# Moving a query block and the early input loads within the order of the projection stage of a hybrid attention / RWKV-7 / MoE block

## The chip, the cores and the metric

One core of a Trainium2 chip runs the whole program. The metric is the device time of one execution in microseconds; each version is given by the median of its runs, with the smallest and the largest beside it.

## What is computed

One layer of an encoder over 2048 tokens of width 1024, cut to what matters here:

```python
h = rmsnorm(x, g_mix) * (1 + sc1) + sh1          # adaLN: sh1, sc1 come from c @ w_ada
pq, pk, pv, pr = split(h @ w_in)                 # one combined input projection
q, k = rope(rmsnorm(pq)), rope(rmsnorm(pk))      # 8 query heads, 2 key heads, 64 wide
o_att = softmax(q @ k.T / 8) @ pv                # all 2048 keys, grouped queries
r, k, v, dw, da, dg = split(centred_shift(pr))   # p + mu * ((prev + next) / 2 - p)
kk = k * k_k / |k * k_k|                         # per head
for each direction:                              # forward and backward
    w  = exp(-0.606531 * sigmoid(w0 + tanh(dw) @ w_up))
    a  = sigmoid(a0 + da @ a_up)
    kd = k * (1 + (a - 1) * k_a)
    y += wkv7_scan(r, w, kd, v, kk, a)           # recurrence over the tokens
    bonus += sum(r * kd * r_k) * v
o_rwkv = (groupnorm(y) * ln_w + ln_b + bonus) * (sigmoid(dg) @ g_up)
x = x + gt1 * concat(o_att, o_rwkv) @ w_out
h2 = rmsnorm(x, g_ffn) * (1 + sc2) + sh2
x = x + gt2 * expert_choice_ffn(h2)              # 16 experts, each takes 256 tokens
```

## The kernel before

The program has stages: the projections (`phase1`), the mixers, in which attention blocks and the recurrence's chunks are interleaved, the output projection, the router and the experts. A mixer's first instructions need the projections' last rows, through DRAM buffers (`d_qk`, `d_x`, `d_v` and others).

**Projections.** `phase1` works on the tokens in two halves of 1024. Of a half, the normalised, modulated input lies on chip transposed, in four pieces of 256 tokens (`hh`, `hl`, a high and a low part, since each product is made of three fp32r products). `project` (L239 to L248) makes 128 output columns for one piece: 8 slices of the inner dimension times 3 products, 24 matmuls (L247) into one PSUM tile `proj_ps`; there are three such buffers. A projection of 128 columns is four of these, 96 matmuls, with weights loaded by `load_w` on SP's queue and split by ScalarE (L148) and GpSimd (L149, `w_lo`). `plain` copies the result out; `shifted` also makes the token shift: one ScalarE row (L263) and two VectorE rows (L265) per piece.

After the key projection and two shifted ones for the decay, rate and gate inputs (blocks 12 and 13), which `phase1` writes out at the start of each half, come the items of a list:

- `q0` to `q3`, **query blocks** (`qk`): four plain projections and `qk_post` (L309), which normalises per head and applies the rotary factors. Its large VectorE rows are L324, L328 and L329, two of each.
- `h0` to `h3`, **recurrence blocks** (`heads`): three shifted projections (`s_r`, `s_k`, `s_v`, 12 pieces) and `prep` (L356), for two quarters of 512 tokens. `prep` begins with head sums on TensorE (`pn`, L275), which become the factor `pb` (L306) of the first VectorE row that all else needs: L378, `kkn`. Then it makes the operands of the recurrence for both directions. Its end is L422 (`pinv`, the last reader of `s_r`), the matmuls `pbo` (L424) and `pg` (L428), and the VectorE rows L426 and L432.
- `x0` to `x2`, **early inputs** (`early`): the next half's `x` for one piece, four loads of 128x512, with their sums of squares on ScalarE (L162), the reciprocal root on VectorE (L165, L166, L55 to L63) and the scaling. `load_xp(half, 3)` follows within v0.
- `v0`, **values** (`values`): a plain projection; in the first half it also makes the second half's pieces (`load_piece`), piece by piece, with that half's key projection.

```python
X_TAGS = [x.split() for x in ("rrkk vvrk vrkv rrkk", "rkrk vrkv vrkv rrkk")]     # L30
xt = self.tpool.tile([P, 512], F32, tag="s_" + tags[2 * i + m], name="xt", bufs=4)   # L159
pair = lambda tag: [self.tpool.tile([P, 512], F32, tag=tag, name=tag, bufs=5 if tag == "p" else 4) for _ in range(2)]
for item in ORDER[half]:                                                         # L579
    dict(q=qk, h=heads, v=values, x=early)[item[0]](int(item[1]))
```

The loads of `x` use buffers of the recurrence blocks: x0 of the second half takes two of the four `s_r` and two of the four `s_k` buffers (tags "rkrk"). A block takes two of each of `s_r`, `s_k` and `s_v`, so two blocks' tiles exist at a time; buffers go round in the order in which the program asks for them.

The order of the list is that in which the instructions are written. A scheduler then places each engine's instructions, by priority and by when their inputs are expected, so that neighbouring items overlap on the engines. On the chip each engine runs its row of instructions in that fixed order, and so does SP's queue.

Of the kernel before, what the change touches and what calls it, by code (L numbers as in the profile page):

```python
# [24 lines left out]
CH = 64  # L25
DSC = 0.606531

ORDER = [x.split() for x in ("h0 q0 h1 q1 h2 h3 x0 q2 x1 q3 x2 v0", "h0 q0 h1 q1 h2 q2 h3 v0 q3")]

X_TAGS = [x.split() for x in ("rrkk vvrk vrkv rrkk", "rkrk vrkv vrkv rrkk")]  # L30

# [6 lines left out]
class Encoder:  # L38
# [397 lines left out]
    def phase1(self):  # L436
# [13 lines left out]
        with ExitStack() as c:  # L450
# [72 lines left out]
            for half in range(2):  # L523
# [54 lines left out]
                ahead, xts = [], []  # L578
                for item in ORDER[half]:  # L579
                    dict(q=qk, h=heads, v=values, x=early)[item[0]](int(item[1]))  # L580
# [1034 lines left out]
```

## Time and profile before

| | before |
|---|---|
| runs (us) | 3757.07, 3762.44, 3744.38 |
| median | 3757.07 |
| profiled execution, its own time | 3751.49 |
| span of its profile | 3749.8 |
| TensorE busy | 94% |
| VectorE busy | 67% |
| mean granted TensorE clock | 0.957 |

The profile is of one execution. Engines are PE (TensorE's matmuls), PEld (its weight loads), DVE (VectorE), ACT (ScalarE), POOL (GpSimd) and SP (the engine that issues most DMAs); busy times are in microseconds and `x` counts instructions. The span is also shown in 40 equal slices, of which each digit is the busy share in tenths; a slice is 93.7 us long, so the projection stage, some 760 us, is the first eight. PEclk is the TensorE clock that was granted, as a share of full speed. In the views of single instructions a row is: start, length, engine, line, operation, result <- operands, shape, and in square brackets how long the engine had been idle before it and what ended that. In the groups by line a row is: line, engine, operation, count | busy time, mean ns of one | idle time just before them, and what ended most of it.

### The profile page before, as it was taken

The numbers are of one execution on the slowest core, as the hardware profiler recorded it, in microseconds if no ns is written. First come the engines' busy times: TensorE is split into PE (matmuls) and PEld (weight loads), VectorE is DVE, ScalarE is ACT, GpSimd is POOL, SyncE is SP. The second block draws the span as 40 slices with busy tenths as digits, with TensorE's granted clock in tenths as the row PEclk, the third lists the DMA queues.
The fourth block names the chain that finished last, engine by engine and source line by source line (L and its number), as shares of the span: only waits on it lengthen the run. The fifth ranks groups of instructions, "written<-read, shape, count | busy, mean of one in ns | idle before, by whom it ended". The sixth has DMA issues, their size and how long they took to land. (4 is left out here: it accounts for less than half of the span.)

```text
span 3749.8 us, 61495 instructions
## 1 busy us (share of the span) xinstructions
PE 3509.9 (94%) x23436; PEld 2856.7 (76%) x23436; DVE 2516.7 (67%) x4289; ACT 1755.2 (47%) x3066; POOL 1512.5 (40%) x1484
## 2 busy tenths in 40 slices
PE   6998899799999999999999997993999999999998
PEld 5887788656666666676666664772999999999997
DVE  6688778876857778558867675447555656655653
ACT  4445444414555555545555564231444444444443
POOL 3445344526263353663364554332332332322321
PEclk8999899879999999999999998996999999999999
DMA  5335334443323433433333232443566766767664
GB/s 182 105 130 168 112 113 141 139 129 73 91 68 79 121 95 85 114 88 87 84 85 85 69 82 82 156 145 113 188 206 205 222 202 216 218 203 222 220 199 127
DMA packets 531228, 510.93 MB, mean 136 GB/s; under 512 B 213304, under 2 KB 449954, under 8 KB 525812
## 3 DMA queue, kind: packets, MB, share of 16 engines
q1 hardware_dynamic: 520612, 472.08, 41.1%
q0 software_dynamic: 10000, 34.91, 4.0%
q8 instruction: 185, 3.03, 0.3%
q14 instruction: 111, 0.91, 0.1%
q10 hardware_dynamic: 320, 0.00, 0.0%
HBM read 392.57 MB, written 109.07 MB: 134 GB/s over the span
## 5 line engine op out<-in xcount | busy, mean ns | idle before, releaser
L1452 DVE TENSOR_TENSOR w_lo<-w_raw,w_hi 128x2048 fp32r<-128x2048 f32 x189 | 432.3, 2293 | 385.8 <-ACT w_hi L1449 385.4
L1516 PE MATMUL gu<-hh,w_lo 128*128 128x256 f32 x2048 | 573.5, 280 | 0.0
L1516 PE MATMUL gu<-hl,w_hi 128*128 128x256 f32 x2048 | 572.7, 280 | 0.0
L1516 PE MATMUL gu<-hh,w_hi 128*128 128x256 f32 x2048 | 572.5, 280 | 0.0
L699 POOL TENSOR_TENSOR acc<-acc,pt 128x512 f32<-128x512 f32 x256 | 354.9, 1391 | 469.0 <-ACT pt L696 456.0
L1449 ACT CAST w_hi<-w_raw 128x2048 fp32r<-128x2048 f32 x192 | 366.9, 1912 | 319.9 <-PE down L1539 133.3
L696 ACT ACTIVATE pt<-st_ps 128x1024 f32<-128x1024 f32 x256 | 262.2, 1024 | 394.8 <-PE st_ps L695 221.2
L649 DVE TENSOR_REDUCE mx<-s_ps 128x1 f32<-128x512 f32 x512 | 342.6, 681 | 149.7 <-PE s_ps L648 148.2
L247 PE MATMUL proj_ps<-hh,w_hi 128*128 128x258 f32 (+1 forms) x1280 | 375.3, 294 | 32.8 <-DVE s_k L265 23.8
L1516 PEld LDWEIGHTS gu<-hh,w_lo 128*128 128x128 f32 x2048 | 388.0, 189 | 0.0
L1516 PEld LDWEIGHTS gu<-hh,w_hi 128*128 128x128 f32 x2048 | 385.6, 188 | 1.3
L1516 PEld LDWEIGHTS gu<-hl,w_hi 128*128 128x128 f32 x2048 | 385.5, 188 | 1.4
L247 PE MATMUL proj_ps<-hl,w_hi 128*128 128x258 f32 (+1 forms) x1280 | 373.0, 292 | 6.4 <-DVE hl L149 5.9
L247 PE MATMUL proj_ps<-hh,w_lo 128*128 128x258 f32 (+1 forms) x1280 | 371.5, 290 | 0.0
L149 POOL TENSOR_TENSOR dl<-hid,dh 128x256 fp32r<-128x256 f32 x128 | 135.1, 1056 | 448.1 <-ACT dh L148 447.8
L686 PE MATMUL o_ps<-pt,av 128*64 128x512 f32 x1024 | 278.5, 627 | 6.7 <-ACT pt L696 6.7
L247 PEld LDWEIGHTS proj_ps<-hh,w_hi 128*128 128x128 f32 x1280 | 250.8, 196 | 41.7 <-issue 23.0
L247 PEld LDWEIGHTS proj_ps<-hl,w_hi 128*128 128x128 f32 x1280 | 251.4, 196 | 10.6 <-DVE hl L149 6.6
L699 DVE TENSOR_TENSOR acc<-acc,pt 128x512 f32<-128x512 f32 x192 | 194.7, 1014 | 91.0 <-ACT pt L696 90.3
L247 PEld LDWEIGHTS proj_ps<-hh,w_lo 128*128 128x128 f32 x1280 | 250.6, 196 | 2.1 <-issue 1.1
L647 PE MATMUL s_ps<-khh,qhl 128*128 128x512 f32 x512 | 240.6, 471 | 9.5 <-DVE mx L649 8.1
L694 PE MATMUL st_ps<-qhl,khh 128*128 128x512 f32 x512 | 229.0, 447 | 2.8 <-ACT pt L696 1.8
(418 smaller groups left out, 8125.1 us busy)
## 6 DMA issues: line engine op xcount, KB each, us to landing
w_raw<-in_w_gate_dram SPq DMA_DIRECT2D x64, 1024.0 KB
w_raw<-in_w_up_e_dram SPq DMA_DIRECT2D x64, 1024.0 KB
w_raw<-in_w_down_dram SPq DMA_DIRECT2D x64, 1024.0 KB
d_x<-X SPq DMA_DIRECT2D x32, 1024.0 KB
xin<-d_x SPq DMA_DIRECT2D x64, 512.0 KB
w_raw<-in_w_in_dram SPq DMA_DIRECT2D x80, 256.0 KB
mod_w<-in_w_ada_dram SPq DMA_DIRECT2D x64, 256.0 KB
mod_w<-in_w_ada_dram SPq DMA_DIRECT2D x8, 1024.0 KB
```

What stands on the lines that cost most here:

```text
L149: (eng or nc.gpsimd).tensor_tensor(out=lo, in0=src, in1=hi.bitcast(F32), op=ALU.subtract)
L247: nc.tensor.matmul(acc[:, :n], a[:, kt, :], b[:, kt, lo : lo + n], start=(kt == 0 and m == 0), stop=(kt == KT - 1 and m == 2))
L647: nc.tensor.matmul(s, qs[h][:, ts], khh[:, ks], start=True, stop=False)
L649: nc.vector.tensor_reduce(out=mx[:, 4 * h + qt, kc : kc + 1], in_=s, axis=AX.X, op=ALU.max)
L686: nc.tensor.matmul(av[64 * h : 64 * h + 64, :], v[:, kb, :], pt[:, h, :], start=(kb == 0), stop=(kb == 15), tile_position=(0, 64 * h))
L694: nc.tensor.matmul(s[:, h, :], khh[:, ks], qs[h], start=True, stop=False)
L696: nc.scalar.activation(out=pt, in_=s, func=AF.Exp, scale=0.125)
L699: eng.tensor_tensor(out=acc[:, h, :], in0=(first if kb == 1 else acc)[:, h, :], in1=pt[:, h, :], op=ALU.add)
L1449: nc.scalar.copy(out=hi, in_=raw)
L1452: eng.tensor_tensor(out=lo, in0=raw, in1=hi.bitcast(F32), op=ALU.subtract)
L1516: nc.tensor.matmul(acc[:, m, :], a[:, kt, i * P : (i + 1) * P], b[:, kt, :], start=(kt == 0 and n == 0), stop=(kt == KT - 1 and n == 2))
```

## The change

One line, the list of items of both halves. In the first half x0 and q2 move ahead of h3, and x1 comes behind h3 as x0 did. In the second half q1 moves from between h1 and h2 to between h2 and h3, and q2 from between h2 and h3 to behind h3.

```diff
-ORDER = [x.split() for x in ("h0 q0 h1 q1 h2 h3 x0 q2 x1 q3 x2 v0", "h0 q0 h1 q1 h2 q2 h3 v0 q3")]
+ORDER = [x.split() for x in ("h0 q0 h1 q1 h2 x0 q2 h3 x1 q3 x2 v0", "h0 q0 h1 h2 q1 h3 q2 v0 q3")]
```

What it moves is seen in the engines' rows. In the names of tiles the number tells one tile from another.

VectorE in the first half, around the last rows of h2 (`pinv_3168`, `cum_3172`), before; `hss_3583` and the rows behind it belong to h3's factor, `ssq_3781` to x0:

```order
L409 SCALAR_TENSOR_TENSOR X_3157<-kkn_3104,ex_3150 128x4x128
L286 TENSOR_SCALAR hss_3583<-pn_3570 128x16
L422 SCALAR_TENSOR_TENSOR pinv_3168<-s_r_2596,prm_cols_295,kd0_3129 128x512
...
L295 TENSOR_TENSOR rp0_109<-hrn_3585,rp0_109 128x8x2
L426 TENSOR_TENSOR cum_3172<-pbo_3170,s_v_2844 128x512
L432 SCALAR_TENSOR_TENSOR cum_3172<-cum_3172,prm_cols_295,pg_3174 128x512
L165 TENSOR_TENSOR ssq_3781<-ssq_3781 128x2
```

The same place in the change; `qk_t1_3380` is q2's, `s_r_3409`, `s_k_3532`, `s_k_3533` and `s_v_3657` are h3's, as are `hss_3796` and `kkn_3827`:

```order
L422 SCALAR_TENSOR_TENSOR pinv_3168<-s_r_2596,prm_cols_295,kd0_3129 128x512
L329 TENSOR_TENSOR qk_t1_3380<-qk_t1_3380,qk_t2_3381 128x512
...
L265 SCALAR_TENSOR_TENSOR s_r_3409<-proj_ps_3504,prm_ex_299,s_r_3409 128x256
L426 TENSOR_TENSOR cum_3172<-pbo_3170,s_v_2844 128x512
L432 SCALAR_TENSOR_TENSOR cum_3172<-cum_3172,prm_cols_295,pg_3174 128x512
L265 SCALAR_TENSOR_TENSOR s_k_3533<-proj_ps_3600,prm_ex_299,s_k_3533 128x256 x2
...
L265 SCALAR_TENSOR_TENSOR s_v_3657<-proj_ps_3752,prm_ex_299,s_v_3657 128x256 x2
...
L286 TENSOR_SCALAR hss_3796<-pn_3783 128x16
...
L378 SCALAR_TENSOR_TENSOR kkn_3827<-s_k_3532,prm_ex_299,pb_3822 128x512
```

Before, h3's shifted projections lay ahead of h2's last rows, and its `hss` was two rows ahead of them; now most of h3's shifts lie behind them, and `hss` and `kkn` behind these.

TensorE at the same place, before; `pn_3570` and `pv_3601` are h3's, `proj_ps_3878` is q2's:

```order
L275 MATMUL pn_3570<-ksq_3567,bones_105 32x128 x8
...
L247 MATMUL proj_ps_3878<-hh_505,w_hi_3814 128x256
L424 MATMUL pbo_3170<-pinv_3168,bblk_98 128x512
L428 MATMUL pg_3174<-sg_762,g_l_119 128x512
L337 MATMUL pv_3601<-ident_60,s_v_3443 128x128 x4
```

And in the change, where `proj_ps_3572` to `proj_ps_3752`, `pn_3783` and `pv_3814` are h3's:

```order
L247 MATMUL proj_ps_3572<-hh_433,w_lo_3535 128x258
L424 MATMUL pbo_3170<-pinv_3168,bblk_98 128x512
L428 MATMUL pg_3174<-sg_762,g_l_119 128x512
L247 MATMUL proj_ps_3600<-hh_505,w_hi_3534 128x258
...
L247 MATMUL proj_ps_3752<-hh_577,w_lo_3659 128x258
L275 MATMUL pn_3783<-ksq_3780,bones_105 32x128 x8
L337 MATMUL pv_3814<-ident_60,s_v_3656 128x128 x4
```

`pn` stood 69 rows ahead of `pbo`; it now stands 146 rows behind it, and 144 of the rows between are L247 rows of h3.

TensorE at the end of the second half, before; `pbo_7875` is the first quarter's of h3, `proj_ps_8198` the last query block's (q3), `p1_8400` the mixers' first row:

```order
L424 MATMUL pbo_7875<-pinv_7873,bblk_98 128x512
L428 MATMUL pg_7879<-sg_4777,g_l_119 128x512
L337 MATMUL pv_7886<-ident_60,s_v_7639 128x128 x4
L247 MATMUL proj_ps_8198<-hl_4624,w_hi_8108 128x256
...
L275 MATMUL pn_8227<-qk_sq_8224,bones_105 32x128 x3
L385 MATMUL lora_ps_7901<-tw_4900,l_hi_7379 128x512
...
L846 MATMUL p1_8400<-xin_8397 128x128 x4
```

And in the change, where `pbo_7785` is h3's, of its last quarter:

```order
L247 MATMUL proj_ps_8198<-hh_4623,w_lo_8109 128x256
L275 MATMUL pn_8227<-qk_sq_8224,bones_105 32x128 x8
L846 MATMUL p1_8400<-xin_8397 128x128 x4
L424 MATMUL pbo_7785<-pinv_7783,bblk_98 128x512
L428 MATMUL pg_7789<-sg_4777,g_l_119 128x512
L337 MATMUL pv_8040<-ident_60,p_7986 128x128 x4
L279 MATMUL pn_8227<-ident_60,hsm_8236 128x128 x2
L846 MATMUL p1_8406<-xin_8397 128x128 x4
```

h3's first quarter ended among q3's projections, and its second quarter's `lora_ps` rows stood behind them; now only h3's very last two matmuls stand behind q3's projections.

## Rows read from the trace of the kernel before

**Rows 1.** The page: busy engines, then TensorE's busy tenths in 40 slices.
```profile
PE 3509.9 (94%) x23436; PEld 2856.7 (76%) x23436; DVE 2516.7 (67%) x4289; ACT 1755.2 (47%) x3066; POOL 1512.5 (40%) x1484
...
PE   6998899799999999999999997993999999999998
```

**Rows 2.** Busy time by stretch of the projection stage (columns in its first line).
```profile
core 0: us, PE busy (x) PEld busy (x) DVE busy (x) ACT busy (x) POOL busy (x), PEclk, DMA share, GB/s
284.00:338.40 54.40, 49.22 (x366) 44.55 (x364) 45.61 (x72) 31.18 (x66) 26.85 (x18) 0.97 0.50 170
338.40:421.50 83.10, 61.32 (x418) 52.20 (x419) 77.19 (x156) 49.42 (x104) 40.10 (x28) 0.84 0.50 165
421.50:481.00 59.50, 59.50 (x505) 59.03 (x507) 29.80 (x62) 21.65 (x43) 16.19 (x12) 1.00 0.21 63
496.30:562.30 66.00, 59.41 (x448) 54.86 (x447) 60.85 (x90) 30.85 (x63) 33.26 (x22) 0.95 0.40 140
562.30:634.00 71.70, 65.74 (x504) 60.82 (x505) 57.36 (x91) 34.51 (x71) 32.82 (x23) 0.95 0.37 129
634.00:697.80 63.80, 58.39 (x447) 53.95 (x447) 58.32 (x91) 30.57 (x62) 32.86 (x22) 0.97 0.37 135
757.50:840.00 82.50, 74.68 (x300) 49.39 (x298) 59.35 (x124) 12.48 (x17) 15.26 (x14) 0.69 0.47 121
```

**Rows 3.** Order of time: the end of h2, first half, and its L422 in the second.
```profile
323.37 1.68 DVE L422 SCALAR_TENSOR_TENSOR pinv<-s_r,prm_cols,kd 128x512 f32<-128x512 f32 x1
325.10 1.13 PE L424 MATMUL pbo<-pinv,bblk 128*128 128x512 f32 x2 [1.29 <-DVE pinv L422]
326.06 1.02 PE L428 MATMUL pg<-sg,g_l 128*128 128x512 f32 x2
...
680.21 0.73 DVE L422 SCALAR_TENSOR_TENSOR pinv<-s_r,prm_cols,kd 128x512 f32<-128x512 f32 x1
```

**Rows 4.** Costliest groups by line, projections and the mixers' start.
```profile
L149 POOL TENSOR_TENSOR w_lo<-w_raw,w_hi 128x512 fp32r<-128x512 f32 x80 | 112.1, 1423 | 173.7 <-ACT w_hi L148 155.7 <-PE pn L275 17.9 <-DMA rope<-in_rope_dram 0.2
L265 DVE SCALAR_TENSOR_TENSOR s_r<-proj_ps,prm_ex,s_r 128x256 f32<-128x256 f32 x64 | 30.5, 479 | 10.0 <-ACT s_r L263 9.4
...
L329 DVE TENSOR_TENSOR qk_t<-qk_t,qk_t 128x512 f32<-128x512 f32 x20 | 18.3, 917 | 1.6 <-POOL qk_t L327 1.5
...
L328 DVE TENSOR_TENSOR qk_t<-qk_sq,rope 128x512 f32<-128x512 f32 x20 | 17.1, 856 | 8.8 <-DMA qk_sq<-qk_xn 8.8
...
L56 DVE TENSOR_TENSOR rsq_t<-hrn 128x16 f32<-128x16 f32 x18 | 8.6, 479 | 0.6
```

**Rows 5.** Busy time by stretch again: a wait of TensorE, and stretches at the lower clock.
```profile
177.50:182.30 4.80, 0.00 (x0) 0.03 (x1) 4.80 (x8) 2.35 (x5) 2.79 (x2) 0.87 0.72 273
182.30:188.00 5.70, 5.70 (x27) 5.70 (x28) 5.70 (x6) 1.13 (x3) 5.60 (x4) 0.51 0.40 129
372.20:396.10 23.90, 12.54 (x62) 9.72 (x63) 23.61 (x50) 13.54 (x29) 12.02 (x8) 0.50 0.42 159
768.00:812.50 44.50, 42.19 (x177) 31.65 (x175) 26.87 (x61) 4.73 (x9) 0.00 (x0) 0.50 0.59 139
```

**Rows 6.** Order of time: the head of the stage's first block, h0.
```profile
129.89 0.65 PE L275 MATMUL pn<-ksq,bones 128*32 128x128 f32 x16
...
145.31 0.75 DVE L378 SCALAR_TENSOR_TENSOR kkn<-s_k,prm_ex,pb 128x512 f32<-128x512 f32 x1 [4.11 <-PE pb L306]
```

**Rows 7.** Order of time: the first and the last row of x0's normalisation on VectorE.
```profile
331.25 0.16 DVE L165 TENSOR_TENSOR ssq<-ssq 128x2 f32<-128x2 f32 x1 [2.66 <-ACT junk L162]
...
339.07 0.65 DVE L63 SCALAR_TENSOR_TENSOR rs<-rsq_t,rs 128x2 f32<-128x2 f32 x1
```

**Rows 8.** Order of time: the last projection, the mixers' first load, their first matmul.
```profile
714.43 0.28 PE L247 MATMUL proj_ps<-hh,w_lo 128*128 128x256 f32 x1
714.65 0.54 SPq L631 DMA_DIRECT2D q_raw<-d_qk  x1
724.35 0.58 PE L846 MATMUL p<-xin 64*128 64x128 f32 x1 [3.44 <-DMA xin<-d_x]
```

## Prediction

> **What bounds the kernel now.** I read the page first, then the busy times stretch by stretch, then the costliest groups of instructions, then the order of time around a few rows. The page shows TensorE busy for 94% of the span and the mixing and expert stages, from the ninth slice on, almost all at nine tenths [rows 1]. The change touches only the projection stage, the first 760 us, so the question is when that stage lets the mixers start; behind that point TensorE is the limit, and I take a shift there as a shift of the end.
>
> Inside the stage the limit is VectorE. In the seven stretches [rows 2], whose bounds are mostly the starts of a recurrence block's first `kkn` row (L378: 284.0 for the first half's h2, 338.4 for its h3; 496.3, 562.3, 634.0 and 697.8 for h0 to h3 of the second half), VectorE is busy for 77.2 of 83.1 us, 60.9 of 66.0, 58.3 of 63.8. Only from 421.5 to 481.0 is TensorE full (59.5 of 59.5) while VectorE has 29.8 us of work: there nothing can start before the new half's projections are made. So blocks put in another order cost VectorE the same work; what can change is how long it waits, and which work stands ahead of the two points that count: the start of the second half's projections (about 419 us, two us before the full stretch) and the start of the mixers.
>
> **First half.** Here a query block moves between h2 and h3, and x0, four loads of inputs, moves ahead of h3 too. The loads take two of the four `s_r` and two of the four `s_k` buffers. Before, h3 took the pair that h1 had freed; now x0 takes that pair, and h3 must wait for the pair of h2. The order shows it: h3's `pn`, which stood 69 rows ahead of h2's last `pbo` on TensorE, stands 146 rows behind it, with 144 projection matmuls (six groups of 24) in between. That `pbo` waits for h2's last L422 on VectorE.
>
> 1. When does L422 end? Before, at 325.0 [rows 3]. It now has a query block's work beside it, but fewer projection shifts. In the second half, where h2 has a query block inside already, 46.9 us pass from kkn to the end of L422 (634.0 to 680.9) [rows 2, 3]; some 8 of the 16 shifts in there (0.48 us each [rows 4]) now come later, which leaves 43, and 283 + 43 = 326. I take 325, no change.
> 2. From there TensorE does `pbo` and `pg`, 2.0 us (325.1 to 327.1) [rows 3], then 144 matmuls. At the full clock 505 matmuls take 59.5 us [rows 2], so 144 take 17.0. Then follows the pattern of the stage's very first block, whose rows have the same order: from `pn` at 129.9 to kkn at 145.3, 15.4 us [rows 6]. h3's kkn comes at 325 + 2.0 + 17.0 + 15.4 = 359.4, where it was at 338.4: 21 later.
> 3. What has left the rest: q2's own VectorE work. Two each of L324 (taken like the first block's kkn, 0.75 us [rows 6]), L328 and L329 (0.86 and 0.92 us) make 5.1 [rows 4], and its eleven rows of 16 columns, 0.48 us at the longest [rows 4], some 3: together 8. Were the moved work to meet GpSimd's at its worst, each of the four L328 and L329 rows would be a little longer; I stay at 8. So 21 - 8 = **+13 us** at the start of the second half's projections.
> 4. TensorE stands idle before that `pbo`: its other work in the interval is gone by then. A 4.8 us wait at 177.5 is followed by 5.7 us at a granted clock of 0.51, with 27 matmuls [rows 5] where the full clock does 48. One such stretch costs half its length, about 3. First half: **+16** (ends: +8, where VectorE's filler work covers half the wait; +31, the first rival).
>
> The rest of the half is moved at no cost. x0's four loads, and the two weight loads of a block with their splits on GpSimd, are issued earlier or later by one block; SP's queue has gaps here, and GpSimd is busy for 26.9 of 54.4 us [rows 2]. If that cover went, a late `w_lo` split would hold TensorE for one, 1.4 us [rows 4]. x0's wait on SP stands ahead of h3's weight loads, and what it waits for is h1's last row, which ends before h3's projections begin.
>
> **Second half.** No input loads compete here. h2 now follows h1 directly, q1 stands between h2 and h3, and q2, v0 and q3 follow h3.
>
> 5. h1 to h2 back to back: the first half's h2 to h3 of before is that case, 54.4 us, of which about 5.3 is x0's normalisation (ten rows between 331.3 and 339.7, the first and the last [rows 7]). So 49, where it was 71.7 with 14.3 of VectorE idle [rows 2].
> 6. h2 to h3 has q1 between: the neighbours are 71.7 (h1 to h2) and 63.8 (h2 to h3) [rows 2]. The order of TensorE's rows at h3's head is that of the 71.7, so I take 71.7. h3's kkn: 49 + 71.7 = 120.8 after h1's, where it was 135.5: 14.7 earlier, of which 8 is the query block now behind it. Gain at equal work: **-7**. With 63.8 it is -15; with the idle time given back in full at h3, 0.
> 7. The tail. After h3 TensorE has three blocks instead of two, so its last projection stays near 714.7, and the mixers' first loads, which came at 714.65 right behind it, stay there too; the first `p1` waited for them until 724.4 [rows 8]. In exchange h3's last row comes some 20 us sooner than 757.5, and the mixers' maxima and masks meet less of it. I price that at nothing: from 757.5 to 840.0 VectorE is idle for 23 of 82.5 us already, and TensorE runs at a clock of 0.69 [rows 2].
>
> **Sum.** +16 - 7 = +9 us. The profiled execution took 3751.49, so 3760.5; the median of the three runs is 3757.07, 5.6 above it, and with the same distance the forecast is **3766 us**, 0.24% more. About 0.5% (19 us) is what a measurement of this kernel can tell from no change, so the forecast is no change.
>
> **The rivals.**
>
> *Slower: the half clock holds through h3's projections.* Place: the 144 matmuls behind h2's last `pbo`. The rows from 372.2 to 396.1 show the half clock for 23.9 us in a stretch in which TensorE was idle for about half of the time [rows 5], and here it comes out of a wait too. All 144 at half the rate cost 17.0 more in place of the 3 counted: first half +30, total +23, 3780. It decides from a clock below 0.6 over those matmuls. Against it: after the single wait the half clock lasted 5.7 us, a third of the 17. The Trainium skill (TensorE: Matmul & The Clock Gate, section "HAM oscillation — how this bites in real kernels") says that each wait between groups of matmuls lets the next group start at half rate; the trace agrees in the stretch after 182.3, and by that alone the sum would lie between mine and this one.
>
> *Faster: the mixers open at the full clock.* From 768.0 to 812.5 TensorE is busy for 42.2 of 44.5 us at a clock of 0.50 [rows 5], so there it is the limit itself. If h3's earlier end leaves it fewer holes and the clock stays up, those 44.5 us shrink to what VectorE needs, 26.9 and some waiting: about -17. With step 6 at its other end (-15) and the 3 us of step 4 not lost the total is 13 - 15 - 17 = -19, 3738. Against it: the first rows still wait for their loads.
>
> *No gate: x0's buffers come free in time.* Then step 2 costs nothing and only the -7 is left: 3750. For it: VectorE, not TensorE, has been the limit. Against it: the 144 matmuls stand behind `pbo` in an order fixed when the program is built, and nothing lets TensorE pass it.
>
> **How the numbers follow.** The forecast 0.53, the half clock 0.25, no gate 0.12, the full clock in the mixers 0.10. So faster by over 0.5%: 0.10; within 0.5%: 0.65; slower by over 0.5%: 0.25. The range goes from 3740, which leaves out the full-clock case, to 3788, the half clock with the second half returning nothing (+30, some 8 below the very worst end): about 2 in 10 stay outside, since the mixers' rows are interleaved anew as well, which no row prices.
>
> **What would show it.** First half: TensorE idle ahead of h2's last `pbo`, h3's kkn near 360 instead of 338.4, the full stretch of projections starting some 13 to 17 us later than 421.5, and its clock between `pbo` and `pn`. Second half: about 49 us from h1's to h2's kkn, near 72 from h2's to h3's. Tail: h3's last row some 20 us earlier against the half's own start, and the clock from 768 on. I am wrong if h3's kkn in the first half stays within 5 us of 338.4, or if the mixers open at the full clock.

## The result: slower by 1.16%, and the profile after

| | before | after |
|---|---|---|
| median (us) | 3751.88 (3744.38 to 3762.44, 4 runs) | 3796.99 (3783.97 to 3807.03, 4 runs) |
| ratio | | 1.0116, 95% interval 1.0092 to 1.014 |
| profiled execution: span | 3749.8 | 3793.3 |
| mean granted TensorE clock | 0.957 | 0.953 |

The change costs 43.5 us (35 to 53), where 9 were forecast, and the time lies above the range. The profiled executions differ by 43.5 us too, so their rows can be read directly. Below, a ratio is turned into microseconds by (ratio - 1) x 3752.

The page of the changed kernel, busy engines and two of its lines of 40 slices:

```profile
PE 3525.7 (93%) x23436; PEld 2868.5 (76%) x23436; DVE 2520.5 (66%) x4289; ACT 1756.4 (46%) x3066; POOL 1520.7 (40%) x1484
...
PE   6998799799999899999999998994999999999998
...
PEclk8998899879999799999999999997999999999999
```

The instructions are the same in number and nearly so in busy time [rows 1]: VectorE has 2520.5 us instead of 2516.7, TensorE 3525.7 instead of 3509.9. What grew is idle time and time at the lower clock. In the line of the clock the 14th slice, 1233 to 1328 us, has a 7: a place far behind the projections.

**First half, as forecast.** The changed kernel in order of time (start, length, engine, line): the end of h2, h3's head sums, h3's `kkn`, and the `kkn` rows of the second half's four blocks:

```profile
326.15 1.35 DVE L422 SCALAR_TENSOR_TENSOR pinv<-s_r,prm_cols,kd 128x512 f32<-128x512 f32 x1
327.56 2.08 PE L424 MATMUL pbo<-pinv,bblk 128*128 128x512 f32 x2 [6.64 <-DVE pinv L422]
349.55 0.65 PE L275 MATMUL pn<-ksq,bones 128*32 128x128 f32 x16
364.97 0.75 DVE L378 SCALAR_TENSOR_TENSOR kkn<-s_k,prm_ex,pb 128x512 f32<-128x512 f32 x1 [4.18 <-PE pb L306]
...
513.67 0.75 DVE L378 SCALAR_TENSOR_TENSOR kkn<-s_k,prm_ex,pb 128x512 f32<-128x512 f32 x1 [4.11 <-PE pb L306]
580.66 0.74 DVE L378 SCALAR_TENSOR_TENSOR kkn<-s_k,prm_ex,pb 128x512 f32<-128x512 f32 x1
634.51 0.73 DVE L378 SCALAR_TENSOR_TENSOR kkn<-s_k,prm_ex,pb 128x512 f32<-128x512 f32 x1
709.99 0.75 DVE L378 SCALAR_TENSOR_TENSOR kkn<-s_k,prm_ex,pb 128x512 f32<-128x512 f32 x1 [4.49 <-PE pb L306]
```

TensorE waits 6.64 us for h2's L422, then come h3's projections, and `kkn` comes at 365.0 instead of 338.4. The second half's first `kkn` is at 513.7, 17.4 later than the 496.3 of before [rows 2]. The same kernel by stretches, around that wait and in the second half:

```profile
core 0: us, PE busy (x) PEld busy (x) DVE busy (x) ACT busy (x) POOL busy (x), PEclk, DMA share, GB/s
320.90:327.60 6.70, 0.06 (x2) 0.04 (x1) 5.79 (x8) 2.03 (x5) 3.41 (x2) 0.68 0.19 72
327.60:331.30 3.70, 3.70 (x5) 1.64 (x6) 3.06 (x7) 1.56 (x3) 0.00 (x0) 0.50 0.86 354
331.30:338.10 6.80, 6.80 (x51) 6.80 (x50) 1.71 (x3) 1.22 (x3) 0.00 (x0) 0.84 0.22 77
338.10:349.50 11.40, 11.40 (x97) 11.31 (x95) 3.87 (x8) 4.10 (x9) 2.54 (x2) 1.00 0.30 94
...
513.70:580.70 67.00, 59.86 (x456) 55.29 (x452) 62.50 (x95) 31.55 (x65) 33.22 (x22) 0.95 0.39 138
580.70:634.50 53.80, 48.76 (x374) 44.93 (x372) 44.65 (x67) 26.88 (x53) 24.64 (x17) 0.97 0.42 143
634.50:710.00 75.50, 65.49 (x475) 59.79 (x472) 62.97 (x95) 35.47 (x73) 35.39 (x24) 0.91 0.36 121
```

Behind the wait the clock is at its lower level for 3.7 us and mixed (0.84) for the next 6.8: 3.7 x 0.5 + 6.8 x 0.16 = 2.9 us lost. In the second half h1 to h2 takes 53.8 us and h2 to h3 75.5, where 49 and 71.7 were forecast.

**The tail, not as forecast.** SP's queue in the changed kernel, in order of time:

```profile
739.79 0.33 SPq L418 DMA_DIRECT2D d_x<-X  x1
741.35 1.20 SPq L326 DMA_DIRECT2D qk_sq<-qk_xn  x2
744.75 0.33 SPq L330 DMA_DIRECT2D d_qk<-qk_t  x1
745.17 2.40 SPq L631 DMA_DIRECT2D q_raw<-d_qk  x4
747.66 0.53 SPq L837 DMA_DIRECT2D xin<-d_x  x1
```

And TensorE there, from the last projection on:

```profile
739.67 0.28 PE L247 MATMUL proj_ps<-hh,w_lo 128*128 128x256 f32 x1
749.42 1.18 PE L275 MATMUL pn<-qk_sq,bones 128*32 128x128 f32 x16 [9.48 <-ACT qk_sq L316]
755.22 1.01 PE L846 MATMUL p<-xin 64*128 64x128 f32 x3 [4.62 <-DMA xin<-d_x]
```

Against before [rows 8] the mixers' first matmul, `p1` (L846), comes 30.8 us later (755.2 against 724.4), and this splits by rows: 17.4 were there at h0's `kkn`; TensorE's last projection is another 7.8 behind (739.95 - 714.71 = 25.2, less 17.4), since 192 of its projection matmuls instead of 118 stand behind h3's `kkn` and take 13.0 us longer, while that `kkn` is only 5.2 sooner against h0's; the first load, which stood right behind that projection, now stands 5.2 behind it, since q2's rotary copy (L326) and store (L330) are ahead of it in SP's queue and wait for VectorE; the way from that load to `p1` is nearly unchanged (10.0 against 9.7). From `p1` to the end another 43.5 - 30.8 = 12.7 us are lost; with the interval of the total, 35 to 53, that is 4 to 22.

### The profile page after: what moved, and what is told of

The parts are those of the page before. It is cut to its first block, busy times and chain, and to the rows that moved or that the text cites. A ratio compares the mean times of both kernels' runs of the same rounds, so it can differ in the third digit from the quotient of the medians.

```text
span 3793.3 us, 61471 instructions
## 1 busy us (share of the span) xinstructions
PE 3525.7 (93%) x23436; PEld 2868.5 (76%) x23436; DVE 2520.5 (66%) x4289; ACT 1756.4 (46%) x3066; POOL 1520.7 (40%) x1484
## 5 line engine op out<-in xcount | busy, mean ns | idle before, releaser
L699 POOL TENSOR_TENSOR acc<-acc,pt 128x512 f32<-128x512 f32 x256 | 363.7, 1425 | 487.2 <-ACT pt L696 466.2
L696 ACT ACTIVATE pt<-st_ps 128x1024 f32<-128x1024 f32 x256 | 262.0, 1023 | 378.1 <-PE st_ps L695 240.9
L247 PE MATMUL proj_ps<-hh,w_hi 128*128 128x258 f32 (+1 forms) x1280 | 377.0, 295 | 35.6 <-DVE s_k L265 28.1
L247 PE MATMUL proj_ps<-hl,w_hi 128*128 128x258 f32 (+1 forms) x1280 | 373.5, 292 | 7.6 <-DVE hl L149 5.6
L247 PE MATMUL proj_ps<-hh,w_lo 128*128 128x258 f32 (+1 forms) x1280 | 371.0, 290 | 0.0
L247 PEld LDWEIGHTS proj_ps<-hh,w_hi 128*128 128x128 f32 x1280 | 251.4, 197 | 45.5 <-ACT pc L394 17.9
L247 PEld LDWEIGHTS proj_ps<-hl,w_hi 128*128 128x128 f32 x1280 | 251.8, 197 | 12.9 <-DVE hl L149 6.2
L247 PEld LDWEIGHTS proj_ps<-hh,w_lo 128*128 128x128 f32 x1280 | 251.1, 196 | 1.7 <-issue 0.6
L699 DVE TENSOR_TENSOR acc<-acc,pt 128x512 f32<-128x512 f32 x192 | 182.5, 951 | 89.8 <-ACT pt L696 89.0
```

Of the source, the lines that this page charges most:

```text
L247: nc.tensor.matmul(acc[:, :n], a[:, kt, :], b[:, kt, lo : lo + n], start=(kt == 0 and m == 0), stop=(kt == KT - 1 and m == 2))
L696: nc.scalar.activation(out=pt, in_=s, func=AF.Exp, scale=0.125)
L699: eng.tensor_tensor(out=acc[:, h, :], in0=(first if kb == 1 else acc)[:, h, :], in1=pt[:, h, :], op=ALU.add)
```

## The experiments

Each kernel is before with the edit shown. "First `p1`" is the start of the first L846 row in its profile, taken against the 724.4 of before; "total" is from the ratio of its runs. "Same rows" counts how many of the mixers' TensorE rows (some 3335 in the program), from their last one back, stand in the order of before: a scheduler places them, and it moves them when the rows ahead of them change. "Free sq", the "reliefs" and the passing over of the attention are explained with their edits below. A `p1` is read from one profile each (723.2 to 724.4 in the three kernels whose projections are those of before); the totals carry the intervals shown, and "total - p1" carries them too.

| kernel | first p1 | total (us) | total - p1 | same rows |
|---|---|---|---|---|
| e1, first half of the change | +16.3 | +15 (8 to 22) | -1 | all |
| e3, q2 between, x0 behind h3 | +7.1 | +8 (2 to 15) | +1 | 3246 |
| e11, x0 alone ahead of h3 | +22.2 | +28 (23 to 33) | +6 | 3246 |
| e18, first half, q2 ahead of h3, free sq | +18.9 | +18 (12 to 24) | -1 | 3036 |
| e17, the change with two reliefs | +24.9 | +30 (23 to 36) | +5 | 3245 |
| e2, second half of the change | +14.7 | +23 (16 to 30) | +9 | 1495 |
| e6, free sq | -4.6 | 0 (-6 to 6) | +4 | 1495 |
| e16, q1 and q2 between, free sq | +1.1 | +7 (3 to 11) | +6 | 1495 |
| the change | +30.8 | +44 (35 to 53) | +13 | 495 |
| e7, q1 and q2 between | +8.4 | +2 (-5 to 8) | -7 | 495 |
| e10, q2's transfers on GpSimd | +10.4 | +26 (18 to 33) | +15 | 495 |
| e5, second half, free sq | +12.1 | +44 (32 to 56) | +31 | 495 |
| e12, q2 alone behind h3 | +7.0 | +28 (19 to 36) | +21 | 95 |
| e8 (16), attention passed over 4 times | -1.1 | +15 (7 to 23) | +16 | 0 |
| e8 (24), passed over 6 times | -1.2 | +21 (12 to 30) | +22 | 17 |
| e9, the change, passed over 6 times | +32.5 | +59 (49 to 69) | +26 | 17 |

### First half: x0, the query block, or both

Three of four cases; before is the fourth. The first half's order alone, e1:

```diff
-"h0 q0 h1 q1 h2 h3 x0 q2 x1 q3 x2 v0"
+"h0 q0 h1 q1 h2 x0 q2 h3 x1 q3 x2 v0"
```

> The first half's order of the change with the second half's order of before. Theory (the gate): x0 holds the pair of s_r and s_k buffers that h1 freed, so h3's projections wait for h2's last L422; in the profile of the change this moved the first kkn of the second half's h0 from 496.3 to 513.7 us. Here it must come at 512 to 516 again, and since the rows of the second half and of the mixers stand in the same order as before, the end moves by the same: +14 to +20 us. Rival (what is lost there is made up later, since the mixers have waits of their own): less than +8 us. Rival (the whole loss of 43.5 us of the profiled execution comes from the first half): +35 us or more.

e11, x0 alone ahead of h3:

```diff
-"h0 q0 h1 q1 h2 h3 x0 q2 x1 q3 x2 v0"
+"h0 q0 h1 q1 h2 x0 h3 q2 x1 q3 x2 v0"
```

> In the first half x0 alone moves ahead of h3; q2 stays behind h3, and the second half is as before. Theory (x0's buffers gate h3; with q2 between alone 7 us were lost at h0's kkn, with both 18): h3's projections wait for h2's last L422 (325) with nothing else to do meanwhile, h3's kkn comes at 352 to 362 instead of 338.4 and h0's kkn of the second half 10 to 20 us later than 496.3; total +8 to +20 us. Rival (the gate costs only in company with the query block): h0's kkn within 5 us of 496.3, total within 6 us.

e3, q2 alone ahead of h3:

```diff
-"h0 q0 h1 q1 h2 h3 x0 q2 x1 q3 x2 v0"
+"h0 q0 h1 q1 h2 q2 h3 x0 x1 q3 x2 v0"
```

> q2 stands between h2 and h3 in the first half, as in the change, but x0 stays behind h3; second half as before. Theory (the gate is x0's buffers, not the query block): h3's first kkn comes some 72 us after h2's, q2's work is then behind us, and h0's kkn of the second half is within 5 us of 496.3, the total within 6 us of before. Rival (a query block between the last two recurrence blocks costs by itself): h0's kkn at 508 or later and +12 us or more.

h0's `kkn` in the second half came at 514.3 (e1), 520.1 (e11) and 503.7 (e3), against 496.3. The waits of TensorE from 270 to 345 us in e11 (for what: us in total, times, longest):

```profile
PE pbo L424 <- DVE pinv L422: 14.6, 2, 11.0
PE proj_ps L247 <- DVE s_k L265: 7.3, 1, 7.3
```

and of before, from 270 to 340:

```profile
PE pbo L424 <- DVE pinv L422: 1.6, 2, 1.3
```

ScalarE's row L263 writes h3's `s_r` into the buffers in question. What it waited for from 240 to 366 us in before, e3, the change (e1 has the same line) and e11, one fence each:

```profile
ACT s_r L263 <- PE proj_ps L247: 0.7, 2, 0.4
```

```profile
ACT s_r L263 <- PE proj_ps L247: 4.8, 2, 2.4
```

```profile
ACT s_r L263 <- DVE pinv L422: 9.6, 2, 5.4
```

```profile
ACT s_r L263 <- DVE pinv L422: 7.8, 2, 5.5
```

With x0 behind h3 it waits for its own projection alone; with x0 ahead of h3 it waits for h2's L422, the last reader of `s_r`.

From h2's to h3's `kkn` VectorE stood idle for 8.8 of 54.4 us before [rows 2]; the same stretch of e11, of e1 and of e3, one fence each:

```profile
282.10:359.80 77.70, 55.10 (x377) 48.86 (x380) 49.48 (x74) 32.23 (x65) 27.33 (x19) 0.82 0.30 105
```

```profile
281.60:363.60 82.00, 65.56 (x493) 60.07 (x491) 58.47 (x92) 34.27 (x70) 33.95 (x22) 0.90 0.36 119
```

```profile
282.70:351.00 68.30, 62.32 (x468) 57.60 (x464) 58.76 (x101) 36.37 (x79) 31.64 (x22) 0.95 0.47 159
```

VectorE is idle for 28.2 us in e11, 23.5 in e1 and 9.5 in e3. So the gate is x0's buffers: with x0 behind h3 the idle time is nearly that of before. x0 alone costs 28 us, more than expected. The query block beside it, work that can be done in the wait, gives back 6 of the 24 us at h0's `kkn`, and 13 of 28 in the total. The query block alone makes h0's `kkn` 7.4 us later, where the theory allowed 5, and the total 8 (2 to 15), where it allowed 6; why is not shown.

### Second half: q1, q2, or both

The second half's order alone, e2:

```diff
-"h0 q0 h1 q1 h2 q2 h3 v0 q3"
+"h0 q0 h1 h2 q1 h3 q2 v0 q3"
```

> The second half's order of the change with the first half's order of before. Theory: h0's kkn stays at 495 to 498; h3's kkn comes some 5 us earlier against it than before, as in the change (196.3 us after h0's instead of 201.5), but at the tail two query blocks stand in a row, the second waits for the first's buffer, and the mixers' first p1 comes 13 us later than before, at 735 to 741 instead of 724; the mixers' rows stand in another order and TensorE loses some 15 to 20 us more at the lower clock between 900 and 1700. Total +20 to +30 us. Rival (as predicted, the second half gains 7): -10 to 0 us. Rival (only the tail's 13 us): +10 to +15 us.

e12, q2 alone behind h3:

```diff
-"h0 q0 h1 q1 h2 q2 h3 v0 q3"
+"h0 q0 h1 q1 h2 h3 q2 v0 q3"
```

> First half as before; in the second half q1 stays where it was and q2 alone moves behind h3. With before, the second half's change and the kernel with both q1 and q2 ahead of h3 this makes the four cases of the two moves. Theory (q2 behind h3 is what costs the 23 us, q1's place nothing): h3's kkn comes earlier, p1 comes 8 to 16 us later than 724.4, and the total is +12 to +28 us. Rival (it is the two moves together): within 8 us of before.

e7, q1 alone moved:

```diff
-"h0 q0 h1 q1 h2 q2 h3 v0 q3"
+"h0 q0 h1 h2 q1 q2 h3 v0 q3"
```

> First half as before; second half with q1 and q2 both between h2 and h3, so that one query block less stands behind h3 than in the change. Theory (the tail: the mixers' first loads stand in SP's queue behind q2's rotary copies and stores, 14 us later): with q2 ahead of h3 again the first load comes within 4 us of 714.65 or, where h3's kkn has moved, some 17 us behind that kkn, and p1 within 6 us of 724.4. In the mixers the rows have the order which the change has from the eighth attention block on; if that order costs by itself, the stretch from the 144th to the 208th exponential row (L696) lasts 375 us or more instead of 365, and the total is +10 to +20 us. Rival (it is the later start alone that costs): the stretch stays at 364 to 369 and the total within 8 us of before. Rival (the query block's place between h1 and h2 is what matters): p1 at 735 or later and +12 us or more.

In the total q1's place costs nothing that can be measured (+2), q2 behind h3 costs 28 by itself and 23 with q1 moved too. That agrees with the theory, and e2's `p1` and total came as expected, though it lost 9 us behind `p1` and not 15 to 20. At `p1` it looks otherwise: q1's move alone makes it 8.4 us later, q2's alone 7.0 (8 to 16 expected), both 14.7. The two moves cost about the same there and add; what sets their totals apart lies behind `p1`, 21 us lost in e12 and 7 gained in e7. e7's `p1` missed the 6 us that were expected, because its h3 came later (`kkn` at 714.3 instead of 697.8) and with it TensorE's last projection (721.7 instead of 714.7). e7's profiled execution was its slowest (3772.42; its median is 3754.08), and its stretch of L696 rows (the attention's exponentials) lasted 390 us: the first theory for that stretch held there, but not for the total.

### The tail's waits

In `qk_post` the swapped copy of a query block is loaded into the one buffer `sq` that the next head also needs; e5 (on e2) and e6 (on before) load it into `qk_t2` instead:

```diff
-            sw = sq[:, q, :]
+            sw = t2
```

> As the second half's change alone, but the query block's swapped copy is loaded into qk_t2 and not into the second use of the one sq buffer, which is then free as soon as the head sums (L275) have read it. Theory (the tail is a chain through sq: q3's pn waits until q2's L328 has read sq): q3's pn comes less than 30 us after q2's pn instead of 40.5, the mixers' p1 at least 10 us earlier than with the second half's change alone, and other heads behind a query block come earlier too, so 15 to 30 us less than that kernel. Rival (VectorE's work and not the buffer sets the tail): p1 within 3 us of that kernel's. Rival (the second quarter now waits for the first's L329, since they share qk_t2): slower than that kernel by 5 us or more.

> Before, with the query block's swapped copy in qk_t2 instead of sq, nothing else. Theory (a block's head behind a query block waits for sq, and VectorE waits with it): in the second half h2's and h3's kkn come some 3 to 6 us earlier each, p1 some 5 to 10 us earlier and the total -4 to -12 us. Rival (the second quarter's copy now waits for the first's L329, which gives it back): total 0 to +8 us. Since the mixers' rows stand in another order too, a part of +-15 us may come from there; the first p1 and the first exponential row tell the two apart.

e10 (on e2) issues q2's copies and stores of the second half from GpSimd:

```diff
-                nc.sync.dma_start(out=sw[i : P : 2, :], in_=xn[1 - i : P : 2, :])
+                (nc.gpsimd if half == 1 and j == 2 else nc.sync).dma_start(out=sw[i : P : 2, :], in_=xn[1 - i : P : 2, :])
...
-            nc.sync.dma_start(out=self.d_qk[j, :, t0 : t0 + 512], in_=t1)
+            (nc.gpsimd if half == 1 and j == 2 else nc.sync).dma_start(out=self.d_qk[j, :, t0 : t0 + 512], in_=t1)
```

> The second half's change alone, but q2's rotary copies and stores of that half (L326, L330) are issued by GpSimd and not by SP, so that the mixers' first loads stand behind h3's stores alone. Theory (SP's queue held them: 729.8 against 714.65 before): the first load of q_raw comes at 723 to 726, right behind h3's store of X that went out at 724.4; p1 still stands behind q3's pn, which waits for sq until 734, so p1 comes at 733 to 737 instead of 739. Rival (the first loads wait for something else than their place in the queue): q_raw at 729 or later. The total is taken to follow p1 and the mixers' order: +10 to +30 us over before, so it tells nothing by itself.

In e5 q3's `pn` comes 32.6 us behind q2's instead of 40.6, so `sq` did hold it; but `p1` gains only 2.6 us instead of 10, as the first rival had it, and the total is 20 us worse than e2, with a loss behind `p1`. In e6 both effects are small and the total is that of before: the expected -4 to -12 did not come. e10's queue, in order of time:

```profile
724.75 0.32 SPq L418 DMA_DIRECT2D d_x<-X  x1
725.16 3.21 SPq L631 DMA_DIRECT2D q_raw<-d_qk  x4
728.47 0.53 SPq L837 DMA_DIRECT2D xin<-d_x  x1
```

The first load left at 725.2, as the theory had it, where e2's left at 729.8 behind L326 and L330: it was its place in SP's queue that held it. `p1` came at 734.8, now held by that load and no longer by q3's `pn`, so that part of the expectation was wrong. The 4.3 us that `p1` gained did not show in the total (+26 against +23).

### The order of the mixers' rows

The mixers' two streams are written alternately, and the attention stream is passed over five times at the start (at every fourth turn up to the 20th). Two kernels on before pass it over four and six times, e9 passes it over six times on the change; the projections stay. Four times:

```diff
-                if len(streams) == 2 and g is streams[1] and n % 4 == 0 and n <= 20:
+                if len(streams) == 2 and g is streams[1] and n % 4 == 0 and n <= 16:
```

> Projections exactly as before; only the interleaving of the mixers' two streams is shifted by one step (the attention stream is passed over four times at the start, not five), which puts the mixers' rows in nearly the order that the second half's change with the swapped copy had. Theory (the order of the mixers' rows has a price of its own, which the change pays since a scheduler rebuilds it behind another tail): p1 at 724 as before, but the stretch from the 144th to the 208th exponential row lasts 373 us or more instead of 365, and the total is +10 to +25 us. Rival (the mixers' order is worth nothing, only their start counts): within 6 us of before.

Six times, on before and on the change:

```diff
-                if len(streams) == 2 and g is streams[1] and n % 4 == 0 and n <= 20:
+                if len(streams) == 2 and g is streams[1] and n % 4 == 0 and n <= 24:
```

> Projections exactly as before; the mixers' interleaving shifted by one step the other way than in the kernel that passed the attention stream over four times (here six). Theory (the order of the mixers' rows has a price of its own that has its best near the order of before): p1 at 724 and the total +5 to +20 us. Rival (a recurrence that is ahead is always better): -5 to -20 us. Rival (the 15 us of the other kernel came from its profile's neighbours and not from the order): within 5 us.

> The change itself, with the mixers' interleaving shifted the other way (the attention stream is passed over six times at the start). Projections as in the change, p1 at 755. Theory (of the change's 43 us some 10 or more come from the order of the mixers' rows): the stretch from the 144th to the 208th exponential row falls from 387.7 to 370 us or less and the total is 10 to 25 us below the change, at +18 to +35 us over before. Rival (only the start of the mixers counts): within 6 us of the change.

With `p1` where it was, the total is 15 and 21 us longer: the order has a price of its own for these two steps away from that of before, one in each direction. The stretch from the 144th to the 208th L696 row, 365 us before, lasted 372 us with four, less than the 373 or more that was expected. e9 was expected to give time back and lost 15 more, so it does not help the change to write the recurrence further ahead.

### The change with before's order of the mixers

e17 is the change with the edits of e5 and of e10; of the list, against before, it has:

```diff
-"h0 q0 h1 q1 h2 h3 x0 q2 x1 q3 x2 v0"
-"h0 q0 h1 q1 h2 q2 h3 v0 q3"
+"h0 q0 h1 q1 h2 x0 q2 h3 x1 q3 x2 v0"
+"h0 q0 h1 h2 q1 h3 q2 v0 q3"
```

> The change, with the swapped copy in qk_t2 and q2's copies and stores of the second half issued by GpSimd. All but some 85 of the first of the mixers' 3334 TensorE rows then stand in the order of before. Theory (the change's 43 us are its later first p1, 31, and the order of the mixers' rows, 13): the mixers' first load comes near 740, p1 at 745 to 751, 20 to 27 us later than before, the stretch from the 144th to the 208th exponential row lasts 364 to 371 us as in before, and the total is +18 to +31 us. Rival (the order is worth nothing, the total follows the projections alone): it falls only by what p1 gains, to +35 us or more.

e18 has the edit of e5 and puts q2 back ahead of h3; e16 is the same with the first half of before. e18:

```diff
-"h0 q0 h1 q1 h2 h3 x0 q2 x1 q3 x2 v0"
-"h0 q0 h1 q1 h2 q2 h3 v0 q3"
+"h0 q0 h1 q1 h2 x0 q2 h3 x1 q3 x2 v0"
+"h0 q0 h1 h2 q1 q2 h3 v0 q3"
```

> The change's first half, and the second half with q1 and q2 both ahead of h3, with the swapped copy in qk_t2: the change but for q2's place behind h3. All but some 300 of the first of the mixers' rows stand in the order of before. Theory (q2 behind h3 makes 25 of the change's 43 us, the first half 15, q1's move nothing): h0's kkn at 512 to 516, p1 at 738 to 748, total +10 to +22 us. Rival (the first half's delay and the tail act together and not one after the other): +30 us or more, or within 6 us of before.

e16:

```diff
-"h0 q0 h1 q1 h2 q2 h3 v0 q3"
+"h0 q0 h1 h2 q1 q2 h3 v0 q3"
```

> First half as before; in the second half q1 and q2 both between h2 and h3, and the swapped copy in qk_t2. The version that the runs so far point to: no query block behind h3 but q3, and heads not held by sq. Theory: p1 at 722 to 730, the mixers' rows mostly in the order of before, total -8 to +5 us: it does not beat before by more than can be measured. Rival (the earlier free sq lets h3 start earlier and the whole tail with it): p1 at 718 or earlier and -10 us or more.

e17, two stretches of the mixers, from the 80th to the 128th and from the 144th to the 208th L696 row (counted from 0):

```profile
1295.20:1655.50 360.30, 344.04 (x2207) 248.28 (x2208) 241.67 (x412) 202.87 (x429) 178.98 (x215) 0.97 0.43 106
1742.50:2108.90 366.40, 361.85 (x2147) 247.05 (x2146) 287.93 (x490) 196.86 (x389) 166.37 (x164) 0.99 0.34 85
```

The same two of the change:

```profile
1280.10:1662.60 382.50, 364.93 (x2255) 268.59 (x2254) 258.01 (x444) 206.17 (x437) 182.70 (x216) 0.92 0.42 103
1749.60:2137.30 387.70, 374.98 (x2208) 255.70 (x2207) 297.57 (x503) 201.99 (x401) 164.43 (x166) 0.96 0.34 84
```

and of before:

```profile
1271.80:1637.90 366.10, 349.66 (x2207) 253.11 (x2208) 241.38 (x412) 202.66 (x429) 178.93 (x215) 0.95 0.43 105
1724.90:2090.10 365.20, 361.88 (x2148) 246.94 (x2147) 287.02 (x490) 196.88 (x390) 164.81 (x164) 0.99 0.34 85
```

With the rows of before these two stretches take no longer than before (360.3 and 366.4 against 366.1 and 365.2), though this is e17's fastest execution (3765.31; its median is 3780.97) and the change's is near its median. By the medians what is left, +30, is the later `p1` (+25) and 5 more. Against the change e17 has 14 us less, of which 6 are its earlier `p1`; the other 8 are not clear of the two intervals (23 to 36 and 35 to 53), and the rival's +35 is within the first. Part of the change's longer stretches is work moved into them (48 and 61 more matmuls than in e17), part a lower clock (0.92 and 0.96 against 0.97 and 0.99) and waits: in the second stretch TensorE is idle for 12.7 us, in e17 for 4.6. e18 came out as expected. e16, the version that the runs pointed to, is 7 us slower than before (3 to 11), a little above what was expected: none of the kernels beats before.

## Why the prediction was wrong

- **Steps 1 to 4, the gate in the first half: right.** +16 was forecast at the second half's start, 17.4 came. L422 ended at 327.5 (325 forecast), `pbo` to `pn` took 22.0 us (19.0 at full clock and 3 for the lower one), `pn` to `kkn` 15.4 (15.4). e1 puts it at +15 in the total, and e3, e11 and ScalarE's wait for L422 show that x0's buffers are the cause. The rival that the lower clock holds through all 144 matmuls is out: 2.9 us were lost. The Trainium skill (TensorE: Matmul & The Clock Gate, section "HAM oscillation — how this bites in real kernels") describes a loop in which the wait for a DMA between groups of matmuls makes the next group start at half rate. The trace agrees at this wait, which is for VectorE: behind 6.64 us the granted clock was 0.50 for 3.7 us, so the start and not the whole group was slow.
- **Steps 5 and 6, h1 to h3 of the second half: too good.** 53.8 and 75.5 us against 49 and 71.7. h3's `kkn` came 129.3 us after h1's, 6.2 sooner than before; less the 8 of query work that now lies behind it this is a loss of 2 instead of a gain of 7. The sum also counted the 7 without a way for it to reach the mixers: step 7 leaves the last projection and the mixers' loads where they were, so by the point that counts in the prediction, the start of the mixers, it came to +16.
- **Step 7, the tail priced at nothing: the step that failed.** It said that TensorE's last projection stays near 714.7 and the mixers' first loads with it. Even against h0's `kkn`, TensorE's last projection came 7.8 us later and the loads 5.2 more. The 7.8 come from step 6: the third block behind h3 costs TensorE 13.0 us, and h3's `kkn` did not come 14.7 sooner to pay for it. The 5.2 come from SP's queue, which has q2's rotary copy and store ahead of the loads. The prediction had named SP's queue for the first half and not followed q2's own transfers past the loads in the second. e10 shows the queue. Of the two moves, e2, e12 and e7 show each to cost some 7 to 8 us at `p1`; in the total only q2's place costs, 23 to 28, and the part of that behind `p1` is not explained. Of the other signs, h3's last row came 12.6 us earlier against h0's `kkn`, where 20 was forecast, and the mixers did not open at the full clock: from the last projection to the first L696 row the granted clock was 0.68, where before had 0.60.
- **"The mixers' rows are interleaved anew, which no row prices": left out of the sum and of the range.** The 12.7 us behind `p1` (4 to 22) go with it. The two e8 kernels show that the order alone can move the time by 15 to 21 us; with the order of before and two reliefs the change costs 30 (e17). In the five kernels with 3036 rows or more as before the total follows `p1` within 6 us, in the three with 1495 it is 4 to 9 above; in the others it is -7 to +31 off, and e7, e10, e5 and the change, which share their last 495 rows with before, spread from -7 to +31. So a moved order is not always dearer, and that the order is what costs the change its 12.7 is argued and not isolated.
- **Taken together**: 17 us from x0's gate and 13 from the tail, both seen in the later `p1`, and 13 behind `p1`, put down to the mixers' order, 43. The two halves add, at `p1` (16.3 + 14.7 = 31.0 against 30.8) and in the total (15 + 23 = 38 against 35 to 53).
- **What stays open**: why one order of the mixers' rows is slower than another. The rows show more idle time and a lower clock in two stretches of single executions, and the runs of one kernel lie 11 to 41 us apart; no experiment took one pair of rows alone. That q2's place costs in e12 mostly behind `p1` and in e2 mostly by the later `p1` is read from one profile each.

## What to carry to other kernels

A load placed early can cost whoever uses its buffers next; ask which block's tiles it takes and who must free them. When an item moves to the end of a stage, follow its stores and copies through the DMA queue: the next stage's first loads may stand behind them. Where a scheduler places the rows, a change in one stage can reorder the next; here one step of interleaving alone was worth 15 to 21 us, about as much as either half of the change (15 and 23). Compare the later stage's order before pricing the earlier one.

## What was not expected of the hardware and the program

One step of interleaving in a stage in which TensorE is busy nine tenths of the time moved the total by 15 and 21 us, both ways to the slower side. And x0 alone ahead of h3 (+28) was dearer than x0 with a query block (+15).
